# A two-layer decoder trunk on one core: up and down weights woven in another order, and seven products moved from one quarter to another

## The chip, the cores and the metric

The kernel runs on one core of one Trainium2 chip. The time is device time in microseconds, the median over several executions of the compiled program. In a profile PE is TensorE (matmul), PEld its weight load, DVE is VectorE, ACT is ScalarE, POOL is GpSimd, and SP is the engine whose queue issues most DMAs.

## The reference, cut to what matters

256 tokens of 2048 channels pass two layers. Each layer has a mixer (causal pooling in layer 0, dilated attention in layer 1), a residual with layer norm, a gated feed-forward part (FFN) with a causal convolution of width 3, and a second residual with layer norm. The change is in the FFN and in one detail at the start of the attention.

```python
def conv_ffn(h, w_up, conv_w, conv_b, w_down):
    u = h @ w_up                                  # (256, 2048) @ (2048, 2*5504)
    up = jnp.pad(u, ((0, 0), (CONV_WIDTH - 1, 0), (0, 0)))
    c = conv_b + up[:, 0:S] * conv_w[0]
    for j in range(1, CONV_WIDTH):
        c = c + up[:, j:j + S] * conv_w[j]
    gate, val = jnp.split(c, 2, axis=-1)
    return (jax.nn.silu(gate) * val) @ w_down     # (256, 5504) @ (5504, 2048)

h = layer_norm(DEEPNORM_ALPHA * h + mix, ln1_g[i], ln1_b[i])
ff = conv_ffn(h, ffn_w_up[i], ffn_conv_w[i], ffn_conv_b[i], ffn_w_down[i])
h = layer_norm(DEEPNORM_ALPHA * h + ff, ln2_g[i], ln2_b[i])
```

In the attention, scores get a mask that depends on the distance of key and query alone; three 128x128 masks are computed once.

## The kernel before, in words

**Precision.** Each fp32 matrix is held as a rounded high part and the low part that is left, and a product is three matmuls: high by high, high by low, low by high. For a weight block ACT casts the high part (`do_split`, L82) and DVE subtracts it to get the low part (L83).

**Units.** All work of TensorE is a list of units, run in order by `run_units`. A unit is one weight block, mostly 512 rows by 512 columns (1 MB), its matmuls, and possibly a `post` that takes the sums out of PSUM. Before a unit's matmuls, `ahead` issues the load of the block five units later (SP queue, three raw buffers, L72) and the split of the block three units later (four buffers). After the matmuls the due entries of `pending` run (`later(n, fn)` makes an entry due n units on), then `post`. So the order of instructions on ACT, DVE and SP follows from the order of units.

**FFN.** `ffn(lay)` cuts the 5504 hidden channels into quarters 0 to 10 of 512 (the last has 384). For each quarter, `up(q)` gives four units for the gates and four for the values; these *up units* keep channels on the partitions. Their sums are taken out by `evac` (ACT copy L577, DVE add L578), convolved by `conv` in three steps that are due one unit after another (L586, L591, L592); gates go through Sigmoid (L615) and a multiply (L616); values are multiplied onto the gates (L672) and split (`split_act`, L286, L290) into `gq[q]`.

The down product has tokens on the output partitions. Quarters are taken in chunks (0 to 2), (3 to 5), (6, 7), (8 to 10), and the 2048 output columns in four column groups of 512. One quarter in one column group is an *item*. It is either an ordinary unit, 24 matmuls with 512 columns (L238 to L240), or *seven products*: the block is seen as 2 by 2 parts and multiplied in Strassen's manner with seven part products instead of eight, 42 matmuls with 256 columns (L227 to L229), in two units "a" and "b" that share one load. For these, `split_sums` makes sums of weight parts and their splits on DVE and ACT (L96 to L109), and `left_sums` makes four sums of parts of `gq[q]` (L647 to L650) with their splits (`rest`, L656, L658). The fourth left sum overwrites a part of `gq[q]` that ordinary items still need. Before the change, quarters 1 to 7 take seven products in all column groups, and quarter 9 in two of them in layer 1.

**Weave.** For the first three chunks, `weave` mixes the items of one column group of a chunk with the four up units of a later half quarter. With three items the order is item, up, item, up, item, up, up; with two items it is item, up, up, item, up, up. After a column group is complete, `early_post` and `tm_post` take the four PSUM banks out (L812 to L842), and three DMAs on the POOL queue add what belongs to the token-major residual `HT` (L271). All eight PSUM banks are in use: four for the items, four for the up units. In layer 0, three units after a column group of the third chunk is complete, `to_features` turns `HT` back (DVE transpose L798 and sixteen small DMAs on the SP queue, L788).

**Buffers.** The split quarters `gq` share seven buffers with the layer's input `XC`, so `free[q]` holds back the split of a chunk's first quarter until the chunk before is done.

**Start of layer 1.** The last steps of layer 0's norm (`lo`, L286), the masks (`masks`, POOL iota L1147, DVE L1152 to L1159) and the first key's evacuation (`norm_evac`) become due around the same units.

Of the kernel before, what the change touches and what calls it, by code (L numbers as in the profile page):

```python
# [9 lines left out]
F32 = mybir.dt.float32  # L10
F32R = mybir.dt.float32r
I32 = mybir.dt.int32
AF = mybir.ActivationFunctionType
# [19 lines left out]
def trunk(ctx: ExitStack, tc: tile.TileContext, x, pool_w_in, pool_w_grp, pool_scale, pool_w_out,  # L33
# [514 lines left out]
    def ffn(lay):  # L548
# [5 lines left out]
        sevens = {q: every for q in range(1, 8)}  # L554
        sets = {1: "A", 2: "B", 3: "C", 4: "A", 5: "B", 6: "A", 7: "BC"[1 - lay], 9: "A"}
        if lay == 1:
            sevens[9] = (0, 2)
        free = {}
# [50 lines left out]
        def gate_chain(q, nb, mode, ps):  # L609
                u = evac(ps, nb, mode)  # L610

                def gated(c):
                    def three():
                        s = u[:, :nb, 2:]
                        A.activation(s, c[:, :nb], AF.Sigmoid)  # L615
                        V.tensor_tensor(c[:, :nb], s, c[:, :nb], OP.mult)  # L616
# [8 lines left out]
        def left_sums(q, s):  # L625
# [13 lines left out]
            if len(sevens[q]) < 4:  # L639
                own = apart()  # L640
            else:
                own = [gq[q][:, 0:2, hl, P:T] for hl in range(2)]
# [7 lines left out]
            V.tensor_tensor(d[3], a12, d[1], OP.subtract)  # L650

            def rest():
                both = f[:, 0:2].rearrange("p s (k t) -> p s k t", k=2)
                vs = [((two[:, :, 0], two[:, :, 1]), both), (xs[q][2], d[2]), (xs[q][3], d[3])]
# [4 lines left out]

            later(1, rest)  # L660

# [5 lines left out]
        def val_chain(q, nb, mode, ps):  # L667
# [14 lines left out]
            after(state["done"] + (0 if q in (2, 5) or (q == 10 and lay == 0) else 1), lambda: conv(u, NF + 4 * q, nb, valued, q == 10))  # L682
# [19 lines left out]
        def weave(us, ks):  # L702
# [44 lines left out]
        for us, ks in zip((vals8,) + up(9) + (gates10,), d):  # L747
            free[9] = weave(us, ks)
# [80 lines left out]
    def tm_post(lay, n, c):  # L829
# [3 lines left out]
        def post(t, ps, half=None):  # L833
# [5 lines left out]
            elif half is None:  # L839
                V.tensor_tensor(y, y, ps, OP.add)  # L840
            else:
# [297 lines left out]
    with tc.tile_pool(name="attn", bufs=1) as ap:  # L1139
# [21 lines left out]
        for i in range(3):  # L1161
            later(6 + i, lambda i=i: masks(i))
# [33 lines left out]
```

## Time and profile before

| what | value |
|---|---|
| median of 3 runs | 2049.06 us (2047.81 to 2050.91) |
| profiled execution | 2047.57 us |
| its span | 2045.8 us |
| PE busy | 2027.3 us (99%) |
| PEld busy | 1810.4 us (88%) |
| DVE busy | 1699.9 us (83%) |
| ACT busy | 1259.2 us (62%) |
| granted TensorE clock | 1.0 throughout |
| waits of PE for another engine or a DMA | 13.7 us |

The span runs from the first to the last instruction of the program on the core. A view of waits names, for an engine, the instruction that waited, what ended the wait, the microseconds in total, the number of waits and the longest. A view of stretches gives for each stretch of the span its length and then, for each engine, busy microseconds and the number of instructions in brackets; after them come the granted clock, the DMA share and GB/s. A view of groups gives, for a line and a shape, the count, the busy microseconds and the mean nanoseconds of one. A timeline gives start, length, engine, line, operation and tiles, with the idle time before in square brackets.

### The profile page before, as it was taken

What the parts mean: (1) busy time and instruction counts of PE and PEld (TensorE: products, weight loads), DVE (VectorE), ACT (ScalarE), POOL (GpSimd) and SP (SyncE); (2) the same over time, 40 slices, a digit from 0 to 9 for tenths busy, and PEclk for the clock granted to TensorE, in tenths of its full rate; (3) what the DMA queues carried; (4) which work ended last, traced back from release to release, by engine and by line L of the source; (5) the groups of instructions that cost most, each with busy time, mean ns of one, the idle gap of its engine ahead of it and who ended that gap; (6) DMA issues with size and microseconds to landing.
All of it is one profiled execution on the core that took longest, in us unless ns stands there. A gap on an engine that the chain in (4) does not pass through costs nothing. (4 is left out here: it accounts for less than half of the span.)

```text
span 2045.8 us, 31252 instructions
## 1 busy us (share of the span) xinstructions
PE 2027.3 (99%) x12532; PEld 1810.4 (88%) x12532; DVE 1699.9 (83%) x2020; ACT 1259.2 (62%) x1679; POOL 75.2 (4%) x112
## 2 busy tenths in 40 slices
PE   9999999999999999999999999999999999999999
PEld 9899988898888898889888888998888889889987
DVE  6759877888899899889856657787888889999998
ACT  6545686666766676667534434477766676767673
POOL 2000000001000100100000000000010001000100
PEclk9999999999999999999999999999999999999999
DMA  8655466667456757765475555557576646666665
GB/s 267 211 190 185 168 215 191 198 215 223 151 194 216 220 179 223 225 216 172 167 219 182 175 182 172 186 183 210 164 242 200 226 135 205 217 216 193 209 208 184
DMA packets 278305, 405.92 MB, mean 198 GB/s; under 512 B 80414, under 2 KB 95668, under 8 KB 277904
## 3 DMA queue, kind: packets, MB, share of 16 engines
q1 hardware_dynamic: 266144, 389.72, 57.3%
q0 software_dynamic: 11584, 13.55, 4.4%
q8 instruction: 98, 1.61, 0.3%
q10 hardware_dynamic: 432, 0.66, 0.1%
q14 instruction: 47, 0.39, 0.1%
HBM read 380.01 MB, written 2.10 MB: 187 GB/s over the span
## 5 line engine op out<-in xcount | busy, mean ns | idle before, releaser
L165 PE MATMUL acc<-xc,wh 128*128 128x512 f32 x3264 | 1153.4, 396 | 1.7 <-DVE xc L286 1.6
L166 PE MATMUL acc<-xc,wl 128*128 128x256 f32 x3264 | 917.4, 281 | 6.1 <-DVE wl L83 5.4
L83 DVE TENSOR_TENSOR wl<-raw,wh 128x2048 fp32r<-128x2048 f32 (+2 forms) x318 | 686.7, 2167 | 241.3 <-ACT wh L82 240.5
L165 PEld LDWEIGHTS acc<-xc,wh 128*128 128x128 f32 x3264 | 615.7, 189 | 145.4 <-issue 2.7
L82 ACT CAST wh<-raw 128x2048 fp32r<-128x2048 f32 (+2 forms) x318 | 572.9, 1810 | 249.9 <-PE acc L165 124.8
L166 PEld LDWEIGHTS acc<-xc,wl 128*128 128x128 f32 x3264 | 615.4, 189 | 11.5 <-DVE wl L83 11.0
L96 ACT CAST wh<-raw 128x1024 fp32r<-128x1024 f32 x116 | 121.0, 1052 | 88.3 <-DVE raw L107 76.3
L97 DVE TENSOR_TENSOR wl<-raw,wh 128x1024 fp32r<-128x1024 f32 x116 | 137.2, 1219 | 7.7 <-ACT wh L96 7.7
L577 ACT COPY ut<-acc 128x256 f32<-128x256 f32 x164 | 55.0, 370 | 139.9 <-DVE u L578 117.2
L103 ACT CAST wh<-raw 128x1024 fp32r<-128x1024 f32 x116 | 90.8, 831 | 56.0 <-DMA raw<-in_ffn_w_down_dram 36.3
L106 DVE TENSOR_TENSOR wl<-raw,wh 128x1024 fp32r<-128x1024 f32 x116 | 105.6, 952 | 8.2 <-ACT wh L103 8.1
L229 PE MATMUL t<-wh,g 128*128 128x256 f32 x344 | 96.8, 281 | 2.3 <-DVE g L658 2.3
L228 PE MATMUL t<-wl,g 128*128 128x256 f32 x344 | 96.8, 281 | 0.0
L227 PE MATMUL t<-wh,g 128*128 128x256 f32 x344 | 96.7, 281 | 0.0
L586 ACT ACTIVATE c<-u,cv 128x256 f32<-128x256 f32 x172 | 89.5, 593 | 3.7 <-DVE u L578 3.7
L228 PE MATMUL s<-wl,xs 128*128 128x256 f32 x308 | 86.8, 282 | 2.1 <-DVE wl L97 2.1
L227 PE MATMUL s<-wh,xs 128*128 128x256 f32 x308 | 86.1, 280 | 0.0
L229 PE MATMUL s<-wh,xs 128*128 128x256 f32 x308 | 86.0, 279 | 0.0
L271 POOL DMA_DIRECT2D ht<-w x24 | 20.3, 848 | 1733.8 <-DVE ht L838 680.6
L591 ACT ACTIVATE a<-u,cv 128x256 f32<-128x256 f32 x172 | 73.5, 499 | 0.0
L591 ACT ACTIVATE u<-u,cv 128x256 f32<-128x256 f32 x172 | 73.4, 499 | 0.0
L109 DVE TENSOR_TENSOR raw<-raw 128x1024 f32<-128x1024 f32 x58 | 71.1, 1225 | 2.0
(273 smaller groups left out, 3449.0 us busy)
## 6 DMA issues: line engine op xcount, KB each, us to landing
raw<-in_ffn_w_up_dram SPq DMA_DIRECT2D x160, 1024.0 KB, 5.0
raw<-in_ffn_w_down_dram SPq DMA_DIRECT2D x80, 1024.0 KB, 5.7
raw<-in_pool_w_out_dram SPq DMA_DIRECT2D x16, 1024.0 KB, 5.0
raw<-in_shared_w_k_dram SPq DMA_DIRECT2D x16, 1024.0 KB, 5.0
raw<-in_attn_w_q_dram SPq DMA_DIRECT2D x16, 1024.0 KB, 5.2
raw<-in_shared_w_v_dram SPq DMA_DIRECT2D x16, 1024.0 KB, 5.7
raw<-in_attn_w_o_dram SPq DMA_DIRECT2D x16, 1024.0 KB, 5.0
raw<-in_pool_w_in_dram SPq DMA_DIRECT2D x12, 1024.0 KB, 5.5
```

The source lines that it names most:

```text
L82: A.copy(wh[i][:, s], r[:, s])
L83: V.tensor_tensor(wl[i][:, s], r[:, s], wh[i][:, s].bitcast(F32), OP.subtract)
L96: A.copy(h[:, :, n], r[:, :, n])
L97: V.tensor_tensor(l[:, :, n], r[:, :, n], h[:, :, n].bitcast(F32), OP.subtract)
L103: A.copy(h[:, k, n], r[:, k, n])
L106: V.tensor_tensor(l[:, k, n], r[:, k, n], h[:, k, n].bitcast(F32), OP.subtract)
L165: PE.matmul(ps[m], h[:, k, c], q[:, k, :, :T], start=st, stop=False)
L166: PE.matmul(ps[m][:, :T], l[:, k, c], q[:, k, 0, :T], start=False, stop=sp and not shifted)
L227: PE.matmul(to, xh, h[:, k, n], start=opens and kk == 0, stop=False)
L228: PE.matmul(to, xh, l[:, k, n], start=False, stop=False)
L229: PE.matmul(to, xl, h[:, k, n], start=False, stop=ends and kk == 1)
L591: A.activation(to[:, m, :], u[:, m, i:i + T], AF.Copy, scale=cv[:, i, j:j + 1])
```

## The change

- `weave` puts two up units ahead of the first item: with three items up, up, item, up, item, up, item; with two items up, up, item, up, up, item. It returns the last unit of every item.
- Quarter 0 takes seven products in column groups 2 and 3 (it had none), quarter 3 in 2 and 3 only (it had all four). For both, the fourth left sum is not made with the other three: `last` makes it from the split parts after the item of column group 1 has run, and then overwrites the part of `gq`.
- `done` holds back the convolution of the values of quarters 4 and 7 until the chunk before is complete.
- The gates use one Silu activation in place of Sigmoid and a multiply.
- In the first chunk a column group of seven products only needs the residual scaled in both halves: DVE does one half with the sum, ACT the other.
- The three masks become due one unit later.

```diff
-        sevens = {q: every for q in range(1, 8)}
-        sets = {1: "A", 2: "B", 3: "C", 4: "A", 5: "B", 6: "A", 7: "BC"[1 - lay], 9: "A"}
+        sevens = {q: every for q in range(8)}
+        sevens[0] = sevens[3] = (2, 3)
+        sets = {0: "C", 1: "A", 2: "B", 3: "C", 4: "A", 5: "B", 6: "A", 7: "BC"[1 - lay], 9: "A"}
...
-                        s = u[:, :nb, 2:]
-                        A.activation(s, c[:, :nb], AF.Sigmoid)
-                        V.tensor_tensor(c[:, :nb], s, c[:, :nb], OP.mult)
+                        A.activation(c[:, :nb], c[:, :nb], AF.Silu)
                         gates[q] = c
...
-            if len(sevens[q]) < 4:
+            if q == 9:
                 own = apart()
             else:
                 own = [gq[q][:, 0:2, hl, P:T] for hl in range(2)]
...
-            V.tensor_tensor(d[3], a12, d[1], OP.subtract)
+            if q not in own_at:
+                V.tensor_tensor(d[3], a12, d[1], OP.subtract)
 
             def rest():
                 both = f[:, 0:2].rearrange("p s (k t) -> p s k t", k=2)
-                vs = [((two[:, :, 0], two[:, :, 1]), both), (xs[q][2], d[2]), (xs[q][3], d[3])]
+                halve([((two[:, :, 0], two[:, :, 1]), both), (one, d[2])] + [(own, d[3])] * (q not in own_at))
+
+            def halve(vs):
                 for v, src in vs:
                     A.copy(v[0], src)
                 for v, src in vs:
                     V.tensor_tensor(v[1], src, v[0].bitcast(F32), OP.subtract)
 
+            def last():
+                f = pools["ffn"].tile([P, 4, 2 + T], F32, name="f", tag="t4")[:, :, :T]
+                d = [f[:, i].rearrange("p (k t) -> p k t", k=2) for i in range(2)]
+                for hl in range(2):
+                    V.tensor_tensor(d[hl], gq[q][:, 2:4, hl, :P].bitcast(F32), two[:, 1, hl].bitcast(F32), OP.subtract)
+                V.tensor_tensor(d[0], d[0], d[1], OP.add)
+                halve([(own, d[0])])
+
             later(1, rest)
+            if q in own_at:
+                at(own_at[q], last)
...
-            after(state["done"] + (0 if q in (2, 5) or (q == 10 and lay == 0) else 1), lambda: conv(...))
+            after(done.get(q, 0) or state["done"] + (0 if q in (2, 5) or (q == 10 and lay == 0) else 1), lambda: conv(...))
...
-            last = None
+            ends = []
             for i, u in enumerate(us):
-                j = i if len(items) > 2 else i // 2 if i % 2 == 0 else len(items)
-                if j < len(items):
+                units.append(u)
+                j = i - 1 if len(items) > 2 else (i - 1) // 2 if i % 2 else -1
+                if j >= 0:
                     units.extend(items[j])
-                    last = len(units) - 1
-                units.append(u)
-            return last
+                    ends.append(len(units) - 1)
+            return ends
...
-            for us, ks in zip(up(q) + up(q + 1), d):
-                free[q] = weave(us, ks)
+            ends = [weave(us, ks) for us, ks in zip(up(q) + up(q + 1), d)]
+            free[q] = done[q + 1] = ends[3][-1]
+            own_at[chunks[n][0]] = ends[1][0]
...
-            free[9] = weave(us, ks)
+            free[9] = weave(us, ks)[-1]
...
+            elif first:
+                V.scalar_tensor_tensor(y[:, parts[half]], y[:, parts[half]], ALPHA, ps[:, :256], op0=OP.mult, op1=OP.add)
+                A.activation(y[:, parts[1 - half]], y[:, parts[1 - half]], AF.Copy, scale=ALPHA)
             else:
                 V.tensor_tensor(y[:, parts[half]], y[:, parts[half]], ps[:, :256], OP.add)
...
-            later(6 + i, lambda i=i: masks(i))
+            later(7 + i, lambda i=i: masks(i))
```

More of the change, by code (lines that the diff above doesn't have):

```diff
@@ L553, in ffn @@
         every = (0, 1, 2, 3)
-        sevens = {q: every for q in range(1, 8)}
-        sets = {1: "A", 2: "B", 3: "C", 4: "A", 5: "B", 6: "A", 7: "BC"[1 - lay], 9: "A"}
+        sevens = {q: every for q in range(8)}
+        sevens[0] = sevens[3] = (2, 3)
+        sets = {0: "C", 1: "A", 2: "B", 3: "C", 4: "A", 5: "B", 6: "A", 7: "BC"[1 - lay], 9: "A"}
         if lay == 1:
             sevens[9] = (0, 2)
-        free = {}
+        free, done, own_at = {}, {}, {}
         def pads():
@@ L680, in valued @@
                 at(free.get(q, 0), three)
-            after(state["done"] + (0 if q in (2, 5) or (q == 10 and lay == 0) else 1), lambda: conv(u, NF + 4 * q, nb, valued, q == 10))
+            after(done.get(q, 0) or state["done"] + (0 if q in (2, 5) or (q == 10 and lay == 0) else 1), lambda: conv(u, NF + 4 * q, nb, valued, q == 10))
         def after(u, fn):
```

## The prediction

> **What bounds the kernel now.** I read the page first, then the waits of PE, then stretches cut at the column groups of the weave. From the page:
>
> ```profile
> span 2045.8 us, 31252 instructions
> PE 2027.3 (99%) x12532; PEld 1810.4 (88%) x12532; DVE 1699.9 (83%) x2020; ACT 1259.2 (62%) x1679; POOL 75.2 (4%) x112
> ```
>
> PE is the bound, so only two things count: how many matmul columns the change adds or takes, and how long PE waits. The waits of PE over the whole span:
>
> ```profile
> PE acc L166 <- DVE wl L83: 5.4, 8, 2.0
> PE t L229 <- DVE g L658: 2.3, 4, 0.7
> PE s L228 <- DVE wl L97: 2.1, 3, 1.5
> PE acc L165 <- DVE xc L286: 1.6, 1, 1.6
> ```
>
> All four end in DVE. Where they lie, and what they really take, is seen from stretches of layer 0: the four column groups of chunk 0, eight up units alone, the four groups of chunk 1, and one group of chunk 2. Then layer 1: the first group of chunk 0, and the sum over the four groups of chunk 1.
>
> ```profile
> core 0: us, PE busy (x) PEld busy (x) DVE busy (x) ACT busy (x) POOL busy (x), PEclk, DMA share, GB/s
> 352.60:391.30 38.70, 38.18 (x238) 34.03 (x237) 33.90 (x39) 25.52 (x34) 2.65 (x3) 1.00 0.67 209
> 391.30:429.30 38.00, 38.00 (x238) 34.07 (x237) 33.47 (x37) 24.44 (x31) 2.56 (x3) 1.00 0.70 217
> 429.30:467.30 38.00, 38.00 (x238) 34.06 (x237) 31.70 (x33) 23.33 (x30) 2.58 (x3) 1.00 0.64 204
> 467.30:505.30 38.00, 38.00 (x238) 34.06 (x237) 33.39 (x39) 26.91 (x34) 2.58 (x3) 1.00 0.63 204
> 505.30:550.30 45.00, 45.00 (x259) 39.26 (x258) 35.80 (x40) 30.57 (x47) 0.00 (x0) 1.00 0.57 191
> 550.30:589.50 39.20, 38.11 (x256) 34.56 (x255) 35.81 (x44) 26.54 (x36) 0.51 (x1) 1.00 0.47 161
> 589.50:628.00 38.50, 38.00 (x257) 34.54 (x256) 36.06 (x40) 25.82 (x36) 2.65 (x5) 1.00 0.65 205
> 628.00:667.30 39.30, 38.09 (x257) 34.50 (x256) 36.98 (x41) 25.04 (x35) 3.31 (x6) 1.00 0.62 201
> 667.30:704.60 37.30, 37.22 (x254) 34.12 (x253) 33.22 (x35) 25.92 (x33) 1.29 (x2) 1.00 0.72 236
> 760.50:793.60 33.10, 32.64 (x214) 29.50 (x213) 31.47 (x35) 22.24 (x31) 2.54 (x5) 1.00 0.78 223
> 1459.80:1498.60 38.80, 38.31 (x239) 34.19 (x238) 33.94 (x39) 25.42 (x34) 2.61 (x3) 1.00 0.67 207
> sum 154.20, PE 151.55 PEld 137.97 DVE 142.07 ACT 103.10 POOL 7.77; mean PE 37.89 PEld 34.49 DVE 35.52 ACT 25.78 POOL 1.94
> ```
>
> An up unit takes 45.0 / 8 = 5.62 us. An ordinary item has the same number of columns, so 5.6. A quiet group of chunk 0 takes 38.0, so seven products take (38.0 - 5 x 5.62) / 2 = 4.95. Without a wait a group of chunk 1 would take 4 x 5.62 + 3 x 4.95 = 37.3, one of chunk 2 32.4. What is lost: chunk 0 0.7 and 0.8 (its first group, each layer); chunk 1 154.3 - 149.3 = 5.0 in layer 0 and 154.2 - 149.3 = 4.9 in layer 1; chunk 2 of layer 0 0.7 in the group shown and 3.5 in its last (the longest waits above, 2.0 on L83 and 1.5 on L97); start of layer 1 1.6. Together 17.2 us. The change can't win more than about that, since the columns stay.
>
> **The change part by part.**
>
> *Columns.* Quarter 0 gains seven products in two groups, quarter 3 loses them in two: 28 items per layer before and after. PE's work: 0. The 24 and 42 matmuls are only dealt out in another order.
>
> *What an item and a gate cost the other engines.* DVE groups of chunk 1 in layer 0, then the gate and left-sum rows of the whole span:
>
> ```profile
> L83 DVE TENSOR_TENSOR wl<-raw,wh 128x2048 fp32r<-128x2048 f32 x16 | 36.3, 2286 | 4.8 <-ACT wh L82 4.8
> L97 DVE TENSOR_TENSOR wl<-raw,wh 128x1024 fp32r<-128x1024 f32 x22 | 26.2, 1220 | 0.0
> L109 DVE TENSOR_TENSOR raw<-raw 128x1024 f32<-128x1024 f32 x11 | 13.5, 1225 | 0.4
> L106 DVE TENSOR_TENSOR wl<-raw,wh 128x1024 fp32r<-128x1024 f32 x11 | 13.4, 1219 | 3.0 <-ACT wh L103 3.0
> L107 DVE TENSOR_TENSOR raw<-raw 128x512 f32<-128x512 f32 x11 | 7.6, 692 | 0.4
> L104 DVE TENSOR_TENSOR raw<-raw 128x512 f32<-128x512 f32 x11 | 7.5, 684 | 1.5 <-DMA raw<-in_ffn_w_down_dram 1.5
> L106 DVE TENSOR_TENSOR wl<-raw,wh 128x512 fp32r<-128x512 f32 x11 | 7.5, 683 | 0.0
> L840 DVE TENSOR_TENSOR ht<-ht,t 128x512 f32<-128x512 f32 x3 | 2.0, 680 | 0.0
> L592 DVE TENSOR_TENSOR c<-c,a 128x1024 f32<-128x1024 f32 x4 | 4.9, 1224 | 1.2 <-ACT a L591 1.2
> L616 DVE TENSOR_TENSOR c<-u,c 128x1024 f32<-128x1024 f32 x20 | 24.4, 1219 | 0.2
> L647 DVE TENSOR_TENSOR f<-c 128x256 f32<-128x256 f32 x15 | 6.3, 419 | 0.0
> L615 ACT ACTIVATE u<-c 128x1024 f32<-128x1024 f32 (+1 forms) x22 | 22.9, 1043 | 3.0 <-DVE c L592 2.3
> L615 ACT ACT_TABLE_LOAD x2 | 2.6, 1283 | 0.0
> ```
>
> Seven products cost DVE 2 x 1.22 + 1.23 + 1.22 + 0.69 + 0.68 + 0.68 = 6.94 us, an ordinary item 2.29: 4.65 us apart, for 0.65 us of PE. That is why chunk 1, with three of them in each group, keeps DVE busy 36 to 37 us out of 37.3 and falls behind, while chunk 0 with two (31.7 to 33.9 out of 38.0) doesn't.
>
> *Quarter 3 ordinary in groups 0 and 1.* DVE in the first two groups of chunk 1 falls from 35.8 and 36.1 to about 31.2 and 31.4. *Quarter 0 in groups 2 and 3.* There it rises from 31.7 and 33.4 to 36.3 and 38.0; off the last comes the split and left sums of quarter 3 (1.22 + 4 x 0.42 + about 1.8 = 4.7, now due with the last item and so running into the eight up units behind, where DVE is busy 35.8 of 45.0). So 36.3 and 33.3 against 37.3 of PE.
>
> *Silu.* Takes away 22 multiplies (L616, 1.22 each, two short): 26 us of DVE, beside other work, of which 1.2 lies in every second group. Silu itself isn't in the trace; the nearest row is the Sigmoid it replaces, same shape, 1.04 on the mean, and the bounds are 0 and one table load (1.28) more at each gate; I take the same. [...]
>
> *Left sums.* Per layer DVE gets quarter 0's set, three sums, and their splits (about 2.4), twice `last` (four 0.42 operations each, 3.4), less 0.8 for quarter 3's fourth: +4.9 us, against 13 saved by Silu. `last` waits for PE to end the ordinary item of group 1, with ACT's copy and then DVE behind it; what queues there is the split four units on, which needs the same item's end for its buffer. I take 0; without that cover it would be 5.6 us at most, twice a layer, less three units of splits in hand.
>
> *Weave order.* Repeated, up-up-item-up-item-up-item is the old order turned by two units, so loads (SP), the three accumulating DMAs (POOL) and the sixteen turning DMAs (SP) keep their distance to the items. Only the ends differ. At the start of chunk 1 quarter 5's fourth left sum was needed after 2 items of seven and two up units, 21.1 us; now after four up units, an ordinary item and one of seven, 33.0. It was late by this:
>
> ```profile
> 573.47 0.42 DVE L658 TENSOR_TENSOR g<-f,g 128x256 fp32r<-128x256 f32 x1
> ```
>
> PE waited 0.5 to 0.7 us for it, four times (2.3 in all); 11.9 us of slack covers that. Next late would be the split of the third item, which DVE now reaches earlier too. In 22.4 us (three up units and the ordinary item) it must do the values of quarter 5 (two convolution adds, a multiply and a split at 1.22 as L592 and L616, four sums at 0.42, their splits about 1.5: 8.1), a split of 2.29, the first half of a split for seven (L104 to L107, 3.3) and an evacuation (four adds of 0.41): 15.3. So all 1.5 of chunk 0's starts go, and of chunk 1's 9.9 I let 8.4 go. What stays, 1.5, is for the third and fourth group, which keep three items of seven (DVE 37.0 and 33.2), but now start with three units of splits in hand, some 11 us (half an item and two up units).
>
> *Chunk 2, layer 0.* The last group is late through DVE and the SP queue together:
>
> ```profile
> 835.58 1.25 DVE L798 STREAM_TRANSPOSE hb<-ht 128x1024 f32<-128x1024 f32 x1 [1.03 <-DMA ht<-u]
> 836.85 4.30 SPq L788 DMA_DIRECT2D h<-hb  x6
> 841.25 0.55 SPq L72 DMA_DIRECT2D raw<-in_ffn_w_up_dram  x1
> ```
>
> The transpose waits for the accumulating DMA, and the loads behind it stand in the SP queue for 4.3 us of small DMAs. That pattern turns with the weave and stays. But the convolution of the up group now falls two units before it, not on it, and a multiply is gone. I let 2.2 of 4.2 go, between 0 and all.
>
> *Masks.* DVE at the start of layer 1:
>
> ```profile
> 974.44 2.29 DVE L83 TENSOR_TENSOR wl<-raw,wh 128x2048 fp32r<-128x2048 f32 x1 [1.70 <-ACT wh L82]
> 976.65 0.22 DVE L1152 CAST idist<-dist 128x128 int32<-128x128 f32 x1
> 978.96 1.22 DVE L286 TENSOR_TENSOR xc<-h,xc 128x1024 fp32r<-128x1024 f32 x1
> ```
>
> L286 ends at 980.2, and PE waited 1.6 us for it, so it was wanted at 978.6. Without the 2.3 us of mask work it ends at 977.9. All 1.6 go. The third mask then follows the query's evacuation instead of preceding it; it is needed only by the scores a unit later.
>
> *New costs.* Chunk 0's groups 2 and 3 now have DVE at 36.3 and 33.3 of 37.3, with the up group's second convolution step and the column group's take-out (five adds of 0.42 and one of 0.68 as L840: 2.8 us) due in the same unit. The price lies between 0 and 5.0 us over both layers (half of what the four such groups of chunk 1 lose); I take 1.5, nearer to 0, as the groups ahead of them leave DVE 4 to 6 us idle each.
>
> *Sum.* 1.5 + 8.4 + 2.2 + 1.6 - 1.5 = 12.2 off the profiled 2047.57: 2035.4. The median of the runs stands 1.5 above that execution, so 2037.
>
> **The rivals.**
>
> *The shortage moves to chunk 0* (chance 0.16). Four groups of the weave still have three items of seven, in pairs. If two in a row are enough to use up the hand, half of chunk 1's loss stays (4.9), and chunk 2 stays whole (4.2). For: the first group of chunk 1 was late within 23 us. Against: it began with 8 us of quarter 5's work in it. Gain 17.2 - 9.1 - 1.5 = 6.6, so 2042.5.
>
> *DVE isn't what is short* (0.09). If the loads with three raw buffers set the pace, the relief changes nothing but the masks and the left sums: gain 3.1, same within what can be told, 2046. For: the 1.5 us in which L104 waited for its DMA. Against: the DMA share of 0.47 to 0.65 in those groups.
>
> *Up banks come free late: slower* (0.09). The next up group starts behind an item of seven now everywhere, 4.95 us after the last up unit, before in chunk 0 behind an ordinary item, 5.6; in that window ACT and DVE must empty four banks. In the old chunk 1 the item ended at 589.5 + 4.95 = 594.45, and the last three of the four adds ended at 594.6, just as PE began the next up group:
>
> ```profile
> 593.53 1.07 DVE L578 TENSOR_TENSOR u<-acc,ut 128x256 f32<-128x256 f32 x3
> ```
>
> If it is late by x at each of 24 group ends, PE loses 24x; the 12.2 gained are gone at x = 0.5 us, and at 0.75 the time is 2055. Against: PE shows no wait for L578, and with DVE ahead the four adds end some 3 us before they are needed.
>
> **How the numbers follow.** The forecast has 0.66, with its own range 2032 (all 17.2 gone) to 2041 (chunk 2 and half the rest of the doubtful terms kept). A measurement here can tell about 0.2%, 4 us. Faster: 0.66 + 0.16 = 0.82, less 0.02 for a forecast that falls short by all its doubtful terms: 0.80. Same: 0.09 + 0.02 = 0.11. Slower: 0.09. The range to be held 8 times in 10 takes in the first rival and part of the second: 2031.5 to 2045.5.
>
> **What would show it.** Right: no PE wait on L658 and none on the mask-delayed L286; the first two groups of chunk 1 at 38.0, the last two at 37.3 to 37.8; groups 2 and 3 of chunk 0 at 37.3 to 38; DVE busy lower by 26 - 9.8 = 16 us; two table loads at the gates. Wrong: PE waits on L83 or L97 in chunk 0, a PE wait on L578, or more table loads on ACT than the rows above have.

## The result and the profile after

The changed kernel takes 2057.7 us on the median (2057.0 to 2061.3, five executions), against 2049.06 before: by the means 1.0046 times as long, with an interval of 1.0032 to 1.0061. The forecast was 2037, faster; it went the other way. From the profile's page of the kernel after:

```profile
span 2055.2 us, 31252 instructions
PE 2027.2 (99%) x12532; PEld 1810.4 (88%) x12532; DVE 1687.6 (82%) x2020; ACT 1257.2 (61%) x1689; POOL 75.2 (4%) x112
```

PE does the same work (2027.2 against 2027.3), and DVE is busy 12.3 us less. So the loss is time in which PE stood still or ran slowly, although the engine that it waits for had become less busy. The waits of PE after, over the whole span (in total, number, longest):

```profile
PE acc L166 <- DVE wl L83: 12.1, 11, 2.0
PE s L227 <- DVE u L579: 3.1, 2, 1.6
PE s L228 <- DVE wl L97: 2.2, 4, 1.6
PE gb L925 <- DVE dg L923: 1.6, 1, 1.6
PE acc L165 <- DVE o L1061: 1.2, 1, 1.2
PE shift L362 <- DVE S L345: 0.9, 1, 0.9
```

The waits for left sums (2.3) and for the delayed L286 (1.6) are gone. Waits for splits (L83) went from 5.4 to 12.1, and waits on L579, L923 and L1061 are new. (Line numbers shift: the evacuation's add is L579 now, the convolution L587 to L593, the left sums' splits L658 and L660, the take-out L825 to L858, the last norm L923 and L925.)

Where this lies is seen when both executions are cut at the same matmuls: the first normed FFN matmul of each layer, the first matmul of quarter 8's gates (the seam of chunks 1 and 2), the first normed matmul of layer 1's mixer, and the first matmul of the closing norm (L918, just ahead of L925). All differences to the kernel before, in us of the profiled executions:

| kernel | start | chunks 0, 1 of layer 0 | chunk 2 and on, layer 0 | attention | chunks 0, 1 of layer 1 | chunk 2 and on, layer 1 | tail | sum |
|---|---|---|---|---|---|---|---|---|
| before, its length | 216.3 | 488.7 | 232.5 | 386.0 | 489.0 | 223.9 | 9.5 | 2045.8 |
| after | -1.1 | -5.1 | +10.4 | -0.4 | -5.3 | +9.0 | +1.9 | +9.4 |
| `old_weave` | -0.6 | -2.4 | -0.5 | -0.4 | -4.5 | -0.4 | 0.0 | -8.7 |
| `gap` | -1.2 | -5.1 | +13.1 | -0.4 | -5.3 | +10.6 | +1.4 | +13.2 |
| `two_old` | -0.1 | -5.1 | +5.3 | -0.3 | -5.3 | +8.6 | 0.0 | +3.2 |
| `mix` | +1.8 | -0.5 | -1.3 | -0.5 | -1.0 | -0.4 | 0.0 | -1.8 |
| `hold1` | -0.3 | -6.6 | +8.4 | +0.1 | -6.7 | +3.7 | +2.0 | +0.7 |
| `gap2` | -0.5 | -5.2 | +6.0 | -0.2 | -5.5 | +6.4 | +1.8 | +2.9 |
| `two_new` | +1.6 | -1.5 | +5.1 | -0.3 | -4.0 | +1.7 | +2.0 | +4.5 |
| `silu` | +1.7 | -2.2 | +0.6 | 0.0 | -2.5 | +0.7 | 0.0 | -1.7 |
| `h_two_old` | +0.2 | -6.6 | +2.0 | -0.3 | -6.7 | +1.4 | 0.0 | -10.0 |
| `h_mid` | +1.8 | -6.6 | +9.8 | -0.4 | -6.7 | +13.0 | 0.0 | +11.0 |
| `h_mix` | -0.2 | -5.5 | -0.4 | -0.2 | -5.5 | -0.4 | 0.0 | -12.2 |
| `masks` | -0.9 | -0.3 | -0.2 | -0.4 | -0.2 | +1.7 | +0.3 | +0.1 |

(The names are those of the experiments below. The start varies by 3 us between executions of the same code, so columns are safer to compare than sums; and a column can move by 1.7 us where the edit gives no cause, as in `masks`, so a single difference under 2 us is not read.) Chunks 0 and 1 won 10.4 us together. Chunk 2 and what follows it lost 21.3.

Time at half clock is in these numbers, and about half of it is lost: after, an L165 matmul with the L166 behind it takes 0.35 us ahead of 743.6 and 0.64 behind it. From the start of layer 0's FFN to the closing norm the granted clock was one half for 23.9 us in `gap`, 20.5 in `h_mid`, 13.7 in `two_old`, 6.8 after and in `mix`, 3.4 in `old_weave`, `hold1`, `two_new`, `silu`, `h_two_old` and `h_mix`, and not at all before, in `gap2` and in `masks`. The last section shows where it fell.

The stretches of layer 0 after, in the columns of the prediction: the four groups of chunk 0 and the four of chunk 1 (each begins with its first item and ends with the two up units behind its last), the seam, and behind it two pairs, each of a stretch in which PE was little busy and of the one that follows at about half the granted clock.

```profile
362.80:400.80 38.00, 38.00 (x239) 34.05 (x238) 34.10 (x39) 25.57 (x35) 2.65 (x3) 1.00 0.55 178
400.80:438.70 37.90, 37.90 (x238) 33.95 (x237) 33.71 (x41) 24.40 (x33) 2.56 (x3) 1.00 0.57 179
438.70:476.00 37.30, 37.30 (x257) 34.43 (x256) 34.44 (x39) 24.98 (x34) 1.07 (x2) 1.00 0.62 204
476.00:513.20 37.20, 37.20 (x256) 34.34 (x255) 31.96 (x35) 21.83 (x25) 1.51 (x2) 1.00 0.73 241
558.20:596.20 38.00, 38.00 (x239) 34.05 (x238) 34.29 (x40) 25.45 (x35) 1.75 (x3) 1.00 0.56 192
596.20:634.10 37.90, 37.90 (x238) 33.95 (x238) 33.70 (x41) 24.57 (x33) 1.84 (x3) 1.00 0.58 179
634.10:672.30 38.20, 37.53 (x256) 34.38 (x255) 35.32 (x40) 23.97 (x33) 1.59 (x2) 1.00 0.66 207
672.30:709.90 37.60, 37.38 (x255) 34.27 (x254) 32.39 (x34) 21.41 (x25) 2.59 (x3) 1.00 0.73 238
705.00:734.00 29.00, 27.75 (x158) 23.93 (x157) 23.89 (x35) 16.77 (x28) 2.58 (x3) 1.00 0.58 178
740.20:743.60 3.40, 1.34 (x6) 0.95 (x7) 3.19 (x2) 3.40 (x6) 0.00 (x0) 1.00 0.73 277
743.60:744.00 0.40, 0.40 (x3) 0.40 (x2) 0.40 (x2) 0.40 (x2) 0.00 (x0) 0.52 0.35 51
842.55:845.95 3.40, 1.42 (x10) 1.05 (x9) 3.40 (x3) 0.00 (x0) 0.00 (x0) 1.00 1.05 280
846.00:847.00 1.00, 1.00 (x5) 0.80 (x4) 0.91 (x1) 0.00 (x0) 0.00 (x0) 0.51 1.03 294
```

Seven of the eight groups stand within 0.1 us of the forecast (38.0, 38.0, 37.3, 37.3 in chunk 0; 38.0, 38.0 and 37.3 to 37.8 in chunk 1); the third of chunk 1, at 38.2, doesn't. In the 29 us from 705 on, at the seam, DVE is busy only 23.9. The same stretch by the clock of the kernel before, and of `hold1` (the work in it differs somewhat: quarter 8's gates begin at 698.9 after, at 705.0 before, at 698.1 in `hold1`):

```profile
705.00:734.00 29.00, 28.92 (x178) 25.46 (x177) 26.87 (x36) 17.82 (x29) 2.58 (x3) 1.00 0.65 200
```

```profile
705.00:734.00 29.00, 29.00 (x173) 25.56 (x172) 26.08 (x37) 20.54 (x34) 2.58 (x3) 1.00 0.59 182
```

So DVE wasn't short of time there: something held it. The timelines of ACT and of DVE after say what (start, length, engine, line; idle before, and what ended it, in brackets):

```profile
706.75 2.08 ACT L587 ACTIVATE c<-u,cv 128x256 f32<-128x256 f32 x4 [4.48 <-DVE f L650]
708.74 0.35 ACT L825 COPY w<-s 128x256 f32<-128x256 f32 x1
708.99 1.91 ACT L82 CAST wh<-raw 128x2048 fp32r<-128x2048 f32 x1
...
715.28 1.71 ACT L592 ACTIVATE a<-u,cv 128x256 f32<-128x256 f32 x4 [3.25 <-DVE g L660]
```

```profile
709.12 0.42 DVE L826 TENSOR_TENSOR w<-w,s 128x256 f32<-128x256 f32 x1 [2.46 <-ACT w L825]
...
717.02 1.23 DVE L593 TENSOR_TENSOR c<-c,a 128x1024 f32<-128x1024 f32 x1 [1.78 <-ACT a L592]
...
733.84 0.41 DVE L579 TENSOR_TENSOR u<-acc,ut 128x256 f32<-128x256 f32 x1
```

At the end of chunk 1 the convolution of quarter 7's values, which `done` now holds back, falls due in the same unit as the left sums of quarter 6. Both take one of the four buffers with the tag "t4". The convolution (L587 on ACT) stands 4.48 us until DVE's left sums give one back (L650), and its second step 3.25 us more (L660). The next instruction on ACT is the copy L825 of the column group's take-out. The sums that it copies are complete at 699.0, but it starts at 708.74, as L587 ends (in `hold1`, where it runs ahead of L587, at 701.31). DVE waits for that (2.46), then for L592 (1.78). The sums of quarter 8's gates, complete after four units of 5.62 from 698.86, at some 721.3 (an estimate), are added up by DVE only from 733.84 on. The timeline of PE after shows what follows:

```profile
734.31 0.39 PE L227 MATMUL s<-wh,g 128*128 128x256 f32 x1 [1.56 <-DVE u L579]
...
740.43 0.50 PE L165 MATMUL acc<-xc,wh 128*128 128x512 f32 x1 [0.48 <-ACT wh L82]
742.76 0.38 PE L166 MATMUL acc<-xc,wl 128*128 128x256 f32 x1 [1.83 <-DVE wl L83]
...
744.36 0.63 PE L165 MATMUL acc<-xc,wh 128*128 128x512 f32 x1
744.79 0.41 PE L166 MATMUL acc<-xc,wl 128*128 128x256 f32 x1
```

The first item of chunk 2 waits for a bank of the gates (1.56); its late end makes the next splits late (0.48 and 1.83); then, from 743.6 on, the granted clock is one half, and a matmul starts 0.43 us behind the one of 512 columns (744.36 to 744.79) instead of 0.23 (742.98 to 743.21).

### The profile page after: what moved, and what is told of

Same layout as the page of the kernel before. It is cut to its first block, busy times and chain, and to the rows that moved or that the text cites. A ratio compares the mean times of both kernels' runs of the same rounds, so it can differ in the third digit from the quotient of the medians.

```text
span 2055.2 us, 31252 instructions
## 1 busy us (share of the span) xinstructions
PE 2027.2 (99%) x12532; PEld 1810.4 (88%) x12532; DVE 1687.6 (82%) x2020; ACT 1257.2 (61%) x1689; POOL 75.2 (4%) x112
## 5 line engine op out<-in xcount | busy, mean ns | idle before, releaser
L165 PE MATMUL acc<-xc,wh 128*128 128x512 f32 x3264 | 1155.8, 396 | 2.2 <-DVE o L1061 1.2
L166 PE MATMUL acc<-xc,wl 128*128 128x256 f32 x3264 | 918.9, 282 | 12.1 <-DVE wl L83 12.1
L83 DVE TENSOR_TENSOR wl<-raw,wh 128x2048 fp32r<-128x2048 f32 (+2 forms) x318 | 687.6, 2168 | 259.5 <-ACT wh L82 257.4
L165 PEld LDWEIGHTS acc<-xc,wh 128*128 128x128 f32 x3264 | 617.4, 189 | 146.1 <-DVE o L1061 1.9
L166 PEld LDWEIGHTS acc<-xc,wl 128*128 128x128 f32 x3264 | 616.9, 189 | 16.3 <-DVE wl L83 15.8
L97 DVE TENSOR_TENSOR wl<-raw,wh 128x1024 fp32r<-128x1024 f32 x116 | 138.9, 1222 | 1.1 <-ACT wh L96 1.1
L587 ACT ACTIVATE c<-u,cv 128x256 f32<-128x256 f32 x172 | 89.5, 594 | 19.1 <-DVE f L650 9.0
L592 ACT ACTIVATE a<-u,cv 128x256 f32<-128x256 f32 x172 | 73.5, 500 | 15.9 <-DVE g L660 6.5
L592 ACT ACTIVATE u<-u,cv 128x256 f32<-128x256 f32 x172 | 73.5, 499 | 0.0
```

The costliest lines, as they stand in the source:

```text
L83: V.tensor_tensor(wl[i][:, s], r[:, s], wh[i][:, s].bitcast(F32), OP.subtract)
L97: V.tensor_tensor(l[:, :, n], r[:, :, n], h[:, :, n].bitcast(F32), OP.subtract)
L165: PE.matmul(ps[m], h[:, k, c], q[:, k, :, :T], start=st, stop=False)
L166: PE.matmul(ps[m][:, :T], l[:, k, c], q[:, k, 0, :T], start=False, stop=sp and not shifted)
L592: A.activation(to[:, m, :], u[:, m, i:i + T], AF.Copy, scale=cv[:, i, j:j + 1])
```

## The experiments

Two theories stood against each other at first. One: the new order of the weave, with the hold that belongs to it, costs at the seam of chunks 1 and 2. The other: the moved sevens or the Silu leave too little of DVE. Each experiment starts from the kernel after, unless it says otherwise. Ratios are to the kernel before.

**The old order, everything else kept.** `weave` puts the item first again, and nothing is held.

```diff
-                units.append(u)
-                j = i - 1 if len(items) > 2 else (i - 1) // 2 if i % 2 else -1
-                if j >= 0:
+                j = i if len(items) > 2 else i // 2 if i % 2 == 0 else len(items)
+                if j < len(items):
                     units.extend(items[j])
                     ends.append(len(units) - 1)
+                units.append(u)
...
-            free[q] = done[q + 1] = ends[3][-1]
+            free[q] = ends[3][-1]
```

> The weave goes back to item first everywhere (and the hold of the values of quarters 4 and 7 with it); the moved seven products, Silu and the later masks stay. Theory (the end of chunk 1 is packed into the up units before chunk 2): no PE wait on L579, none in chunk 2 of layer 1, where the changed kernel loses 9 us; chunk 1 loses 1 to 4 us per layer instead of 5; 2040 to 2046 us. Rival (the two-item order itself is what costs): the same, since that order is undone as well. Rival (the moved seven products or Silu cost): at least 2054.

Measured: 2040.35 us, 0.9951 (0.9939 to 0.9964). The loss of chunk 2 is gone in both layers, and of the 10.4 won in chunks 0 and 1, 6.9 stay. So order and hold are the whole loss, and sevens, Silu and masks together are a gain. With its hold, the new order is worth 3.5 us in chunks 0 and 1.

**Eight up units at the seam.** The values of quarter 8 run ahead of chunk 2, so that its start has more room.

```diff
-        units.extend(gates8)
+        units.extend(gates8 + vals8)
         gates10, vals10 = up(10)
-        for us, ks in zip((vals8,) + up(9) + (gates10,), d):
-            free[9] = weave(us, ks)[-1]
+        for us, ks in zip(up(9) + (gates10,), d):
+            weave(us, ks)
+        units.extend(d[3])
+        free[9] = len(units) - 1
```

> The changed kernel, but with eight up units instead of four ahead of chunk 2's weave (gates and values of quarter 8), quarter 9 and the gates of quarter 10 woven in the new order, and the last column group of chunk 2 left bare. Theory (packed end of chunk 1): the PE wait on L579 at the first item goes, chunk 2 of layer 1 up to its last group loses under 2 us; the bare group may cost 2 to 4 us per layer; 2042 to 2049. Rival (the two-item order itself): the waits on L83 in chunk 2 stay, at least 6 us in layer 1; 2054 or more.

Measured: 2063.59, 1.0063 (1.0051 to 1.0076). The time is where the rival put it, though by another wait than the one it named (L83). The largest of its waits of PE:

```profile
PE s L228 <- DVE wl L97: 9.1, 3, 4.3
```

The wait on L579 is gone, so the room at the start does cure that one. But the last column group then has its two items side by side with no up unit between, and that costs more (4.3 us in one wait for L97, whose splits belong to seven products, 6.94 us of DVE against 2.29 for an ordinary item). What was won at one end of the chunk was lost at the other, and some 12 us are lost to the half clock (half of 23.9, an estimate), so this says little on the size of either.

**Two items in the old order.** Chunk 2 alone puts the item first; the hold stays.

```diff
-                units.append(u)
-                j = i - 1 if len(items) > 2 else (i - 1) // 2 if i % 2 else -1
+                first = len(items) > 2
+                if first:
+                    units.append(u)
+                j = i - 1 if first else i // 2 if i % 2 == 0 else -1
                 if j >= 0:
                     units.extend(items[j])
                     ends.append(len(units) - 1)
+                if not first:
+                    units.append(u)
```

> The changed kernel with item first again in chunk 2 alone. Four up units now lie between the last item of chunk 1 and the first of chunk 2 instead of six. Theory (packed end of chunk 1): the start of chunk 2 gets worse, PE waits on L579 or on the left sums of quarter 7 of 4 us or more at the first items of each layer, 2057 to 2070. Rival (the two-item order itself): better, under 2046.

Measured: 2050.9, 1.0006 (0.9997 to 1.0015).

```profile
PE acc L165 <- DVE u L579: 8.0, 2, 4.6
PE s L228 <- DVE wl L97: 4.8, 2, 2.4
```

Neither expectation held in full. With the item two units earlier the seam is worse, as the theory said, 4.6 us in one wait instead of 1.6. Yet the whole is 6.8 us faster than after, and the tail's loss is gone. So there seem to be two costs: one at the seam, which an earlier item makes worse, and one in the rest of chunk 2 that comes with the two-item order itself.

**Up units first in chunk 0 only.** Chunks 1 and 2 have the item first, and only quarter 4's convolution is held.

```diff
-        def weave(us, ks):
+        def weave(us, ks, up_first=False):
...
-            ends = [weave(us, ks) for us, ks in zip(up(q) + up(q + 1), d)]
-            free[q] = done[q + 1] = ends[3][-1]
+            ends = [weave(us, ks, n == 0) for us, ks in zip(up(q) + up(q + 1), d)]
+            free[q] = ends[3][-1]
+            if n == 0:
+                done[q + 1] = free[q]
```

> Up units first in chunk 0 alone; chunks 1 and 2 item first, as before; moved seven products, Silu, masks as changed. Theory: chunk 0 loses nothing, chunk 1 about 1 us per layer (quarter 5's fourth left sum is again wanted after some 22 us), chunk 2 as before or better; 2037 to 2043. Rival (two-item order): the same. Rival (moved seven products or Silu): at least 2054.

Measured: 2045.52, 0.9976 (0.9967 to 0.9986). That is above the 2037 to 2043 expected: chunk 2 is as before, but chunks 0 and 1 won only 0.5 and 1.0. The waits:

```profile
PE t L229 <- DVE g L660: 4.9, 2, 2.5
PE t L227 <- ACT g L658: 1.2, 2, 0.6
```

With chunk 1 item first, quarter 5's fourth left sum comes late again, and by more than before (2.5 us at the longest, against 0.7), now that quarter 4's convolution is held ahead of it. The hold costs at the seam of chunks 0 and 1 too where the order doesn't leave room for it.

**The held convolution one unit later.** It then falls due in the unit behind the left sums, not with them.

```diff
-            after(done.get(q, 0) or state["done"] + ...
+            after(done.get(q, -1) + 1 or state["done"] + ...
```

> The changed kernel with the held convolution (values of quarters 4 and 7) due one unit later, after the split and the left sums of the quarter before have given back their two buffers of the shared four. Theory (the held convolution stands on ACT waiting for those buffers, and the splits queue behind it): ACT's waits of 4.5 and 3.3 us at the end of chunk 1 go, the PE wait on L579 at the first item of chunk 2 falls under 0.5 us, and the stage from quarter 8's gates to the end of layer 1 loses at least 4 of the 10.8 us it lost; 2044 to 2052 us. Rival (there is simply too much DVE work in those six up units): the same or worse, 2056 to 2062.

Measured: 2045.52, 0.9982 (0.9973 to 0.9991), 12.2 us less than after. PE has no wait from 700 to 745. The timelines of ACT and of DVE in `hold1`:

```profile
705.50 2.08 ACT L587 ACTIVATE c<-u,cv 128x256 f32<-128x256 f32 x4 [2.00 <-DVE f L650]
...
711.46 1.71 ACT L592 ACTIVATE a<-u,cv 128x256 f32<-128x256 f32 x4 [0.94 <-DVE g L660]
```

```profile
726.54 0.41 DVE L579 TENSOR_TENSOR u<-acc,ut 128x256 f32<-128x256 f32 x1
```

ACT's two waits fall from 4.48 and 3.25 to 2.00 and 0.94 us, and the gates are emptied 7.3 us earlier (6.6 if counted from their first matmul). DVE's work is the same, so the rival, too much of it in those units, falls: it was the collision that held DVE there. The profiled executions stand 8.8 us apart: of the columns, 5.3 less in chunk 2 of layer 1, 2.0 in that of layer 0, and 2.9 in chunks 0 and 1, where the held convolution of quarter 4 moves too. What stays in chunk 2 is the other cost.

**Old order in chunk 2, with eight up units at the seam.** Both orders item by item: three items new, two items as in `two_old`, and all of quarter 10 woven, so that only two up units are left behind the last item, where after has four and before six.

```diff
-        units.extend(gates8)
-        gates10, vals10 = up(10)
-        for us, ks in zip((vals8,) + up(9) + (gates10,), d):
+        units.extend(gates8 + vals8)
+        for us, ks in zip(up(9) + up(10), d):
             free[9] = weave(us, ks)[-1]
-        units.extend(vals10)
```

> Three-item weave as changed, two-item weave item first, and eight up units alone (gates and values of quarter 8) between chunk 1 and chunk 2 instead of four; quarter 10's values are woven into the last group instead of standing alone at the end. Differs from two_old in those up units only. Theory (what decides is the room between the last item of one chunk and the first of the next): the waits on L579 (8.0 us in two_old) and L97 there go, chunk 2 stands within 2 us of the kernel before in both layers; 2036 to 2043 us. Rival (the loss comes from the new end of chunk 1 itself, whatever follows): at least 2048.

Measured: 2050.46, 1.0002 (0.9993 to 1.0011).

```profile
PE s L228 <- DVE wl L97: 3.9, 4, 1.6
PE t L229 <- DVE xs3Q L660: 1.8, 1, 1.8
PE gb L927 <- DVE dg L925: 1.5, 1, 1.5
```

No wait on L579 and none at the seam, but chunk 2 loses 6.0 and 6.4 all the same, most of it at its end, and the tail loses 1.8. The time is where the rival put it, but the waits are not at the end of chunk 1, which it blamed. And this is the old order. So the new order as such isn't needed for such a loss; what was taken here at that end are the up units behind the last item.

**New order in chunk 2 only.** Three items in the old order, nothing held.

```diff
-                units.append(u)
-                j = i - 1 if len(items) > 2 else (i - 1) // 2 if i % 2 else -1
-                if j >= 0:
+                first = len(items) < 3
+                if first:
+                    units.append(u)
+                j = (i - 1) // 2 if first and i % 2 else -1 if first else i
+                if 0 <= j < len(items):
                     units.extend(items[j])
                     ends.append(len(units) - 1)
+                if not first:
+                    units.append(u)
...
-            free[q] = done[q + 1] = ends[3][-1]
+            free[q] = ends[3][-1]
```

> Three-item weave item first as before, two-item weave up units first; eight up units between the two. Differs from old_weave in chunk 2 alone. Theory (room between the chunks): chunk 2 loses no more than 2 us per layer against old_weave, 2039 to 2044. Rival (the two-item order puts take-out and convolution into one unit and costs by itself): at least 4 us per layer, 2048 or more.

Measured: 2050.91, 1.0003 (0.9994 to 1.0012), above the theory's 2039 to 2044 and where the rival put it.

```profile
PE shift L362 <- DVE S L345: 2.7, 1, 2.7
PE gb L929 <- DVE dg L927: 1.7, 1, 1.7
```

Against `old_weave`, from which only the two-item order differs, chunk 2 of layer 0 loses 5.6 us, that of layer 1 2.0 and the tail 2.0. Both waits shown lie behind the chunk: DVE carries work on past the last item, and the first thing that needs DVE at once, the shift matmuls of the next mixer or the closing norm, waits for it. PE's waits for splits (L83) between 700 and 950 rose too, 3.4 against 2.0, so a cost inside the chunk, as the rival has it, isn't excluded.

**Silu alone**, put into the kernel before.

```diff
-                        s = u[:, :nb, 2:]
-                        A.activation(s, c[:, :nb], AF.Sigmoid)
-                        V.tensor_tensor(c[:, :nb], s, c[:, :nb], OP.mult)
+                        A.activation(c[:, :nb], c[:, :nb], AF.Silu)
```

> The kernel before with Silu for Sigmoid and multiply, nothing else. If DVE's lack of time is what makes PE wait in chunk 1 and in chunk 2 of layer 0, 26 us less of DVE work give 2 to 5 us (the chunk 0 starts keep their 0.7); if not, within 1 us of the kernel before. Two table loads at the gates either way.

Measured: 2043.82, 0.9965 (0.9953 to 0.9978), 5.7 less than the median before. In the profiled execution, the slowest of the five, it wins 2.2 and 2.5 in chunks 0 and 1, where DVE was short, and nothing clear elsewhere.

**Both cures together**: `hold1` and the weave of `two_old`, whose edits are shown above.

> The held convolution one unit later, three-item weave up units first, two-item weave item first: four up units between chunk 1 and chunk 2, six behind the last item of chunk 2. Theory (two separate costs: the hold at the end of chunk 1, and two up units taken from behind the last item of chunk 2): both are gone, chunks 0 and 1 gain 6.6 us per layer, chunk 2 to the end of each layer within 2 us of the kernel before; 2034 to 2040 us. Rival (six up units between the chunks are needed whatever the hold): the waits on L579 of two_old stay in part, 2043 or more.

Measured: 2037.47, 0.9937 (0.9924 to 0.9949), 8.0 less than `hold1`. From `hold1` on, chunk 2 and behind it goes from +8.4 to +2.0 in layer 0 and from +3.7 to +1.4 in layer 1, and the tail from +2.0 to 0.0. Its longest waits:

```profile
PE acc L166 <- DVE wl L83: 3.8, 4, 2.0
PE acc L165 <- DVE u L579: 1.8, 2, 1.0
```

**An order between the two**, on `hold1`: up, item, up, up, item, up in chunk 2, with five units behind the last item.

```diff
-                j = i - 1 if len(items) > 2 else (i - 1) // 2 if i % 2 else -1
+                j = i - 1 if len(items) > 2 else i // 2 if i % 2 == 0 else -1
```

> As h_two_old, but each item of chunk 2 stands between its two up units (up, item, up, up, item, up): five up units in front, five behind. Theory (what counts is the room behind the last item): between hold1 and h_two_old in chunk 2, a loss of 1 to 4 us per layer, tail 0 to 1.5 us late; 2038 to 2043. Rival (take-out and convolution due in one unit): the order of due steps is as in neither, and nothing between the two follows.

Measured: 2056.7, 1.0036 (1.0024 to 1.0049). This was meant to give a point between six and four, and it doesn't, as its rival said:

```profile
PE acc L165 <- DVE w L826: 12.2, 5, 3.9
```

A new wait came in: with an up unit at both ends of a group, the next up group follows on with no item between, and its first matmuls wait for the take-out of the column group. Only its tail can be read: 0.0 with five units behind, as with six.

**Old order from chunk 1 on**: `hold1` and the edits of `mix`.

> The held convolution one unit later; up units first in chunk 0 alone. Differs from mix in the hold of quarter 4's values. Theory (hold): mix lost 4 us per layer at the third item of chunk 1 because the held convolution had pushed all of quarter 5's steps back; that loss falls under 1.5 us, so chunks 0 and 1 gain 4 to 6 us per layer and chunk 2 stays as before; 2036 to 2041. Rival (eight up units in place of ten between chunk 0 and chunk 1): the waits on L660 and on the copies of L658 stay.

Measured: 2035.31, 0.9925 (0.9911 to 0.9938), the fastest here, faster than both kernels. Against `mix`, one unit in the due time of one convolution is worth 10.2 us, and by the profiled executions 9.5 of it in chunks 0 and 1; chunk 2 costs what it cost before.

**Masks alone**, put into the kernel before.

```diff
-            later(6 + i, lambda i=i: masks(i))
+            later(7 + i, lambda i=i: masks(i))
```

> The kernel before with the masks one unit later, nothing else. The forecast: the wait of 1.6 us on L286 at the start of layer 1 goes, nothing comes. What the changed kernel's trace suggests instead: it goes, and a wait of about 1.2 us on the attention's output (L1045) some 55 us later comes, so the attention stage gains 0.4 us.

Measured: 2047.66 once, beside a median of 2049.7 for the kernel before; no ratio. Of its waits:

```profile
PE t L229 <- DVE g L658: 2.4, 4, 0.7
PE acc L165 <- DVE o L1045: 1.2, 1, 1.2
```

The 1.6 us on L286 are gone, and a wait of 1.2 for the attention's output has come. Left: 0.4 us. The 1.7 more in chunk 2 of layer 1 has no cause in the edit that I can name, and stays open.

## Why the prediction was wrong

**The step that failed** is "Weave order", in the sentence "Only the ends differ". It then priced one end, the start of chunk 1. Of the others, two decided:

- *The hold.* `done` stood in the change, and the working has no term for it. It puts a convolution into the unit in which left sums of the same buffer tag are due, and ACT's wait of 4.48 us becomes one of 2.46 on DVE. Moving it by one unit, and quarter 4's with it, gives 12.2 us back on the medians (8.8 in the profiled executions). No step followed ACT's queue through the seam: ACT is busy 61% of the span, but what counted is that its wait of 4.48 us held up the copy behind it, from 699.0 to 708.74. This is shown by `hold1` and its timelines.
- *The two-item order.* It takes two up units from behind the last item, four left instead of six. With the hold out of the way that costs 8.0 us (`hold1` against `h_two_old`, which differ in this order alone). How it costs them is shown only in part. That it is the number of units behind is supported by `gap2`, where two units behind the last item of the old order lose as well, and by the tail: 0.0 with five or six behind in each kernel of the table but `masks` (0.3), 1.4 to 2.0 with fewer. But leaving out one wait of 2.0 (L83) that both have, PE waits over both layers in `hold1` 5.5 us behind chunk 2's last item and 7.8 inside the chunk, in `h_two_old` 0.0 and 3.9. So 3.9 of the 9.4 lie inside, ahead of the last item, and what causes those stays open; the point between, `h_mid`, fell to another wait.

The rest of the new order, in chunk 1, is not clearly a gain: from `h_two_old` to `h_mix`, which has chunk 1 item first and no hold there, the median falls by 2.2 us, less than the five executions of either scatter; in the profiles chunks 0 and 1 lose 2.3 and chunk 2 wins 4.2.

In chunk 2 of layer 0 the waits of PE between 700 and 950 are 10.1 us after, 3.9 before: 6.2 of the 10.4 lost. Two stretches at half clock, 6.8 us, make some 3.4 more (half of them, an estimate); the last section has them.

**The other terms.** *Columns*, 0: right. *Chunks 0 and 1*: forecast 1.5 + 8.4 - 1.5 = 8.4 off, measured 10.4, without a wait for a left sum; of the groups only the third of chunk 1 is longer than said, and the price of chunk 0's last groups, 1.5, was 0. DVE's load by group was not as said: 34.3 and 33.7 us in the first two groups of chunk 1, not 31.2 and 31.4, and 34.4 and 32.0 in the last two of chunk 0, not 36.3 and 33.3. That `h_two_old` comes out at the forecast is partly luck: it won 13.3 in chunks 0 and 1, and in chunk 2 of layer 0 it lost 2.0 where 2.2 were to be won. *Silu* as Sigmoid: right, as the group rows after show, 1042 ns against 1043, and two table loads as before:

```profile
L615 ACT ACTIVATE c<-c 128x1024 f32<-128x1024 f32 (+1 forms) x22 | 22.9, 1042 | 33.3 <-DVE c L593 33.1
L615 ACT ACT_TABLE_LOAD x2 | 2.6, 1283 | 0.0
```

*DVE's busy time* was forecast 16 lower. The times of its instructions add up to 16.1 less (multiplies 26.3 less, left sums 9.8 more), as said; the profile's busy time, which counts the overlap of neighbours once, is 12.3 lower.

*Chunk 2, layer 0*, forecast -2.2: the new order, on which the argument rested, adds other waits instead. With Silu and the moved sevens in the old order it is -0.5 (`old_weave`), with waits of 2.8 against 3.9; the -0.5 includes a stretch of 3.4 us at half clock, some 1.7 lost (an estimate), which the kernel before was spared behind the same wait. *Masks*, forecast 1.6: measured 0.4 or so. The step looked as far as the scores one unit later; a wait came back 60 us on, in the attention, where DVE had stood 4.2 us for a DMA ahead of the work that PE wanted (before it stood 4.0 there, and PE didn't wait). Two rows of DVE's timeline after:

```profile
1035.82 0.98 DVE L1036 STREAM_TRANSPOSE pb<-p 128x768 f32<-128x768 f32 x1 [4.21 <-DMA pTs<-pb]
...
1038.89 0.74 DVE L1061 TENSOR_TENSOR o<-o 128x256 fp32r<-128x256 f32 x2
```

**The rivals.** *The shortage moves to chunk 0* is what the moved sevens do in the old order: in `old_weave` PE waits 1.7 us for splits (L83) in chunk 0 of layer 0, and chunks 0 and 1 win 2.4 there, not 5.1. The new order cured it. *DVE isn't what is short* fell: Silu alone, which takes work from DVE only, wins 4.7 in chunks 0 and 1. *Up banks come free late*, the slower one, named the right row, a PE wait on the evacuation's add, but put it at each of 24 group ends. It came at two places, the start of chunk 2 in each layer, 3.1 us in all, and the banks were late because DVE had been held, not because of the 0.65 us less between last up unit and next group that the rival priced. The chance of 0.09 for slower was the price of that one mechanism; the hold and the room behind the last item had no rival and so no chance at all.

Three readings in the working are off, without weight for the sum: of the four waits on L658 two stand in chunk 0, not at quarter 5; the DMA share in chunk 1's groups reaches 0.72, not 0.65; and masks and left sums make 1.6 + 2.3 = 3.9, not 3.1.

## What to carry to other kernels

Price every line of a change, and at a seam above all the due times: list for each unit what falls due in it and which buffers of which tag it takes, because here a wait of 4.48 us for a buffer, on an engine at 61%, held up the copy behind it and, through that, DVE for 2.46. A rotation of a repeated order wasn't free at its ends: what stood behind the last item was where the late engine caught up, and taking two of six units from there cost 8.0 us (`hold1` against `h_two_old`) and showed up in the next stage (a wait of 2.7 for L345 in `hold1`). An engine that is less busy can still be later, as DVE was: 12.3 us less busy, while PE's waits rose from 13.7 to 24.0. Read where it stands idle and for whom.

## What the runs showed of the hardware

A short pause can cost more than itself. In the kernel before, waits of up to 2.0 us left the granted clock at 1.0 (its one drop, at 2044.91, lies behind the last matmul). After, it fell to one half at 743.61 and at 846.01, for 3.41 us each, which loses some 1.7 us each time (half of 3.41, an estimate). The rows of the stretches above show PE busy for 1.34 and 1.42 us of the 3.40 ahead of the drops. Ahead of the first PE paused twice, for 0.48 and 1.83; ahead of the second once, for 2.0 (L83, 845.3). The two drops lie 102.40 us apart, 30 times the 3.413 that each lasted.

The same pause isn't always followed by a drop. At the seam of layer 1 the kernel after has the two pauses once more, 0.47 and 1.82, and its clock stays at 1.0. The 3.41 us that end with the second pause, in layer 0, then in layer 1 with the 3.41 behind them:

```profile
739.34:742.75 3.41, 1.11 (x7) 0.59 (x5) 2.34 (x2) 3.41 (x6) 0.00 (x0) 1.00 0.83 297
1851.40:1854.81 3.41, 1.12 (x8) 0.60 (x6) 2.35 (x2) 3.41 (x6) 0.00 (x0) 1.00 0.80 297
1854.81:1858.22 3.41, 3.41 (x20) 3.01 (x21) 3.41 (x3) 3.41 (x6) 0.00 (x0) 1.00 0.68 225
```

`old_weave` has the same wait of 2.0 at the same matmul as the kernel before; its clock fell, that of the kernel before didn't. The 3.41 us that end with this wait, before, with the 3.41 behind them; then in `old_weave` the 3.41 ahead of the drop and the 3.41 from it on:

```profile
845.23:848.64 3.41, 1.43 (x12) 1.10 (x10) 3.38 (x4) 1.48 (x1) 0.00 (x0) 1.00 0.91 208
848.64:852.05 3.41, 3.41 (x20) 3.01 (x21) 1.85 (x2) 1.75 (x2) 0.00 (x0) 1.00 0.97 231
```

```profile
841.04:844.45 3.41, 1.43 (x9) 1.02 (x9) 3.41 (x3) 1.47 (x1) 0.00 (x0) 1.00 0.91 228
844.45:847.86 3.41, 3.41 (x13) 2.93 (x12) 1.23 (x2) 1.97 (x2) 0.00 (x0) 0.50 0.97 228
```

PE was busy for 1.43 us in both. What decides whether the clock falls is not shown by these runs. So the same wait of 2.0 came with some 1.7 us more (half of 3.41, an estimate) in `old_weave` and with none before, and two kernels of this case can differ by that much with the same pauses.
